# Layer norm by halves in a two-layer decoder trunk: squares about each half's own mean, and an earlier transpose

## The chip, the cores and the metric

The kernel runs on one core of a Trainium2 chip. The metric is the device time of one execution in microseconds (us). Before the change it is 533.94 us, the median of 3 runs (533.82 to 534.5).

## The reference

Two post-norm layers over 256 tokens of width 1024, in fp32. Layer 0 has a mixer with sparse attention, layer 1 one with stick-breaking attention; each layer ends in a hierarchical mixture of experts. Behind the mixer and behind the experts stands a layer norm, four in all:

```python
def layer_norm(x, g, b):
    xf = x.astype(jnp.float32)
    mu = jnp.mean(xf, axis=-1, keepdims=True)
    var = jnp.mean(jnp.square(xf - mu), axis=-1, keepdims=True)
    return ((xf - mu) * lax.rsqrt(var + LN_EPS) * g + b).astype(x.dtype)
...
    for layer in range(DEPTH):
        ...
        x = layer_norm(DEEPNORM_ALPHA * x + mix, ln_mix_g[layer], ln_mix_b[layer])
        ffn = hierarchical_moe(x, moe_w_grp[layer], moe_b_grp[layer], ...)
        x = layer_norm(DEEPNORM_ALPHA * x + ffn, ln_ffn_g[layer], ln_ffn_b[layer])
```

The experts of a token are chosen from logits of the normed `x` (a group of four, then two experts in it).

## The kernel before, in words

The 256 tokens are two tiles of 128, one token in each partition, with the 1024 features along the free axis. A tile's features are handled in two halves of 512, because the result of a product fills one bank of PSUM (`acc`, 128 x 512). TensorE (PE) makes all products and transposes; VectorE (DVE) and ScalarE (ACT) move and convert results; SyncE (SP) issues the transfers of weights.

A norm has two helpers. `ln_sum` (L340) adds the residual: one `scalar_tensor_tensor` (L344) for each half writes `r = ALPHA*r + acc` and, as a second small instruction, the half's sum to a column of the tile `st`; L346 makes the negative mean of both. `ln_rstd` (L349) lets ACT square each half about the common mean (L353, with the sum of the squares as a second small instruction), then come small DVE steps on one element of each partition: L354 and L355 make the variance, ACT takes Ln and Exp (L356, L357), and L358 to L360 are one Newton step for the inverse root. A norm is made at four places:

- **the route** (`ln_route`, L446, once in each layer's mixer). `proj` adds the last products of the output projection (`out_proj`, L396 to L398), first for tile 0, then for tile 1, half by half. Between them PE transposes the summed `x` of a tile (`mk_xT`, L420, by `transp4`, L309, four 128 x 128 transposes in one PSUM buffer, copied to `rT` by DVE, L314, or ACT, L316). `logits` (L459) multiplies `rT` with the router's weights (L464), copies the four partial results (`part`, L469) and sums them by a product with `sel` (L470). `finish` (L475) corrects the logits by mean and inverse root (L478, L479), `norm` (L481) scales `x` on ACT, and `router` (L945, first step L973) ranks the logits. The gather of tokens (L1231) waits for the ranks. The PSUM buffers of the transposes come from a pool of two.
- **the middle** (`ln_tile`, L363), behind the experts of layer 0, tile 0 and then tile 1. Between `ln_sum` and `ln_rstd` DVE makes `u` of 1024 elements (L372). For tile 0 PE runs 30 small keep-warm products (L370, L327). L381 makes the normed halves, `done` transposes each (L309) and ACT copies them to `xT` (L316). PE then multiplies `xT` with a block of layer 1's weights (`proj_whole`, L254) before it goes on to layer 1's other projections (L266 to L268).
- **the end** (`fin`, L1559), both tiles together, with `u` in L1569 and the result in L1574 and L1575.

Each engine works its instructions off in the order of its own list. The order within a list is set by a scheduler when the program is built. `tc.issue_after(i)` holds what is issued in it behind instruction `i` in that order; `last[...]` keeps such instructions.

A second copy of the program with dense experts follows behind a branch and is not executed here.

Of the kernel before, what the change touches and what calls it, by code (L numbers as in the profile page):

```python
# [9 lines left out]
F32 = mybir.dt.float32  # L10
# [4 lines left out]
OP = mybir.AluOpType  # L15
# [18 lines left out]
def trunk(ctx, tc, io):  # L34
# [301 lines left out]
    def after_ln():  # L336
        with tc.issue_after(last["A"]), tc.issue_after(last["V"]):
            yield

    def ln_sum(r, accs):  # L340

        st = sm.tile([128, 8], F32, name="lnst")
        for h in range(2):
            V.scalar_tensor_tensor(r[:, h * 512:h * 512 + 512], r[:, h * 512:h * 512 + 512], ALPHA, accs[h],  # L344
                                   op0=OP.mult, op1=OP.add, accum_out=st[:, h:h + 1])
        last["m"] = V.tensor_scalar(st[:, 2:3], st[:, 0:1], st[:, 1:2], -1.0 / D, op0=OP.add, op1=OP.mult).ins  # L346
        return st

    def ln_rstd(r, accs, st):  # L349

        nmu, ve, rs, nt = st[:, 2:3], st[:, 3:4], st[:, 4:5], st[:, 5:6]
        for h in range(2):
            last["S"] = A.activation(accs[h], r[:, h * 512:h * 512 + 512], AF.Square, bias=nmu, accum_out=st[:, 6 + h:7 + h]).ins  # L353
        V.tensor_scalar(nt, st[:, 6:7], 1.0 / D, EPS, op0=OP.mult, op1=OP.add)  # L354
        V.tensor_scalar(ve, st[:, 7:8], 1.0 / D, nt, op0=OP.mult, op1=OP.add)  # L355
        A.activation(rs, ve, AF.Ln)  # L356
        last["A"] = A.activation(rs, rs, AF.Exp, scale=-0.5).ins  # L357
        V.tensor_scalar(ve, ve, -0.5, None, op0=OP.mult)  # L358
        V.tensor_scalar(nt, ve, rs, rs, op0=OP.mult, op1=OP.mult)
        last["R"] = V.tensor_scalar(rs, nt, 1.5, rs, op0=OP.add, op1=OP.mult).ins  # L360
        return rs

    def ln_tile(t, r, accs, gb, u, done, warm=0):  # L363


        gt, bt = gb[:, 0], gb[:, 1]
        with tc.issue_after(last["V"] if t else last["lo"]):
            st = ln_sum(r, accs)
        if warm:
            keep_warm(warm, pmt)  # L370
        with (tc.issue_after(last["V"]) if t else nullcontext()):
            last["u"] = V.scalar_tensor_tensor(u, r, st[:, 2:3], gt, op0=OP.add, op1=OP.mult).ins  # L372
        with tc.issue_after(last["u"]):
            rs = ln_rstd(r, accs, st)
        if warm:
            p = pmt()
            for _ in range(2):
                PE.matmul(p[:, 0:256], identf, rs.to_broadcast([128, 256]), start=True, stop=True)
        for h in range(2):
            hs = slice(h * 512, h * 512 + 512)  # L380
            last["V"] = V.scalar_tensor_tensor(r[:, hs], u[:, hs], rs, bt[:, hs], op0=OP.mult, op1=OP.add).ins  # L381
            done(h)
# [37 lines left out]
    def mk_xT(x, xT, t, pool=None, dve=0):  # L420
        for g in range(2):
            mk_xT_half(x, xT, t, g, pool, g < dve)
# [23 lines left out]
    def ln_route(l, x, a, oT, wo, xo, rT, pool):  # L446
# [40 lines left out]
        sts[0] = ln_sum(x[:, 0], a[0])  # L487
        proj(1, (0,))
        mk_xT(x, rT, 0, pool, 1)
        proj(1, (1,))  # L490
        logits(0)
        rss[0] = ln_rstd(x[:, 0], a[0], sts[0])
        norm(0)
        sts[1] = ln_sum(x[:, 1], a[1])
        with tc.issue_after(last["m"]):
            mk_xT(x, rT, 1, pool, 2)
            last["E"] = last["C"]
        rss[1] = ln_rstd(x[:, 1], a[1], sts[1])
        logits(1)
        finish(0)  # L500
        finish(1)
# [1001 lines left out]
    def program(sparse):  # L1503
# [55 lines left out]
        def fin(t, a, gb, u):  # L1559
# [7 lines left out]
            for k in range(NT):  # L1567
                with tc.issue_after(last["m"]):
                    V.scalar_tensor_tensor(box1[k][1], x[:, k], sts[k][:, 2:3], gb[:, 0], op0=OP.add, op1=OP.mult)  # L1569
            rs = [ln_rstd(x[:, k], box1[k][0], sts[k]) for k in range(NT)]  # L1570
            for k in range(NT):
                for h in range(2):
                    hs = slice(h * 512, h * 512 + 512)
# [79 lines left out]
```

## Time and profile before

| | us |
|---|---|
| median of 3 runs | 533.94 |
| the profiled execution | 533.85 |
| its span, first to last instruction | 531.9 |
| PE busy | 501.4 (94%) |
| DVE busy | 289.5 (54%) |
| ACT busy | 220.8 (42%) |

The span is the profiled execution without what lies around the first and the last instruction, 1.95 us. The busy times overlap, since the engines work side by side; PE's matmuls are pipelined, so its 94% is no measure of how near it is to its peak. Times in rows are counted from the start of the span.

### The profile page before, as it was taken

The numbers are of one execution on the slowest core, as the hardware profiler recorded it, in microseconds if no ns is written. First come the engines' busy times: TensorE is split into PE (matmuls) and PEld (weight loads), VectorE is DVE, ScalarE is ACT, GpSimd is POOL, SyncE is SP. The second block draws the span as 40 slices with busy tenths as digits, with TensorE's granted clock in tenths as the row PEclk, the third lists the DMA queues.
The fourth block names the chain that finished last, engine by engine and source line by source line (L and its number), as shares of the span: only waits on it lengthen the run. The fifth ranks groups of instructions, "written<-read, shape, count | busy, mean of one in ns | idle before, by whom it ended". The sixth has DMA issues, their size and how long they took to land.

```text
span 531.9 us, 8516 instructions
## 1 busy us (share of the span) xinstructions
PE 501.4 (94%) x3201; PEld 316.4 (59%) x3201; DVE 289.5 (54%) x824; ACT 220.8 (42%) x433; POOL 7.6 (1%) x18
## 2 busy tenths in 40 slices
PE   8899989999999999999899999999999999999980
PEld 6687656676676354543354996898777454363320
DVE  5878796849669621221166555555648861141125
ACT  4545645547556121121144347556747321131022
POOL 1000000000020000000000000000002000000000
PEclk9999999999999999999999999999999999999995
DMA  8999500009938999999997980003976599999952
GB/s 243 381 429 429 217 0 1 1 0 393 412 152 322 415 363 335 421 422 422 432 430 307 370 341 1 0 1 147 427 297 238 224 394 342 402 423 419 427 217 84
DMA packets 25536, 150.02 MB, mean 282 GB/s; under 512 B 3472, under 2 KB 4112, under 8 KB 14992
## 3 DMA queue, kind: packets, MB, share of 16 engines
q1 hardware_dynamic: 25488, 149.41, 70.1%
q8 instruction: 27, 0.44, 0.3%
q14 instruction: 21, 0.17, 0.1%
HBM read 148.35 MB, written 1.05 MB: 281 GB/s over the span
## 4 chain that ended last, share of the span: by engine, by line
PE 82%; DVE 9%; ACT 4%; DMA 2%; issue 1%; SPq 0%; ACTq 0%; DVEq 0%
PE pmt L1264 16%; PE pmt L1296 9%; PE pmt L1231 4%; PE acc L1305 3%; PE acc L246 3%; PE acc L245 3%; PE acc L398 3%; PE acc L244 3%; PE acc L396 3%; PE acc L397 3%; PE acc L254 3%; DMA wb<-w 2%; PE acc L268 2%; PE acc L266 2%; PE acc L267 2%; PE z L880 2%
## 5 line engine op out<-in xcount | busy, mean ns | idle before, releaser
L1264 PE MATMUL pmt<-wgu,xg 128*64 128x512 f32 (+1 forms) x512 | 92.8, 595 | 0.0
L1264 PEld LDWEIGHTS pmt<-wgu,xg 128*64 128x64 f32 (+1 forms) x512 | 27.2, 123 | 52.9 <-issue 50.8
L190 ACT ACTIVATE wh<-wb 128x1024 fp32r<-128x1024 f32 (+2 forms) x44 | 41.1, 944 | 37.4 <-PE acc L267 19.7
L193 DVE TENSOR_TENSOR wl<-wb,wh 128x512 fp32r<-128x512 f32 (+1 forms) x72 | 45.1, 660 | 19.0 <-ACT wh L190 18.9
L1296 PE MATMUL pmt<-wd,hT 128*64 128x512 f32 (+1 forms) x256 | 53.9, 597 | 0.9 <-ACT hT L1280 0.9
L198 DVE TENSOR_TENSOR yl<-pmt,yh 128x512 fp32r<-128x512 f32 x20 | 13.8, 690 | 47.5 <-ACT yh L190 47.5
L246 PE MATMUL acc<-wl,xhl 128*128 128x512 f32 (+1 forms) x96 | 37.7, 395 | 1.5 <-DVE wl L193 1.5
L244 PE MATMUL acc<-wh,xhl 128*128 128x512 f32 (+1 forms) x96 | 37.3, 389 | 1.4 <-ACT wh L190 1.4
L245 PE MATMUL acc<-wh,xhl 128*128 128x512 f32 (+1 forms) x96 | 37.0, 386 | 0.0
L1272 DVE SCALAR_TENSOR_TENSOR hh<-pmt,cs,silu 128x256 f32<-128x256 f32 x12 | 5.8, 484 | 56.8 <-ACT silu L1270 56.8
L1270 ACT ACTIVATE silu<-pmt 128x256 f32<-128x256 f32 x12 | 4.6, 384 | 76.1 <-PE pmt L1264 76.1
L190 ACT ACTIVATE yh<-pmt 128x512 fp32r<-128x512 f32 x20 | 11.9, 597 | 55.9 <-PE pmt L1296 55.9
L1296 PEld LDWEIGHTS pmt<-wd,hT 128*64 128x64 f32 (+1 forms) x256 | 15.3, 123 | 27.0 <-issue 24.9
L1231 PEld LDWEIGHTS pmt<-Poh,xhl 128*128 128x128 f32 x192 | 24.4, 188 | 5.3 <-issue 3.2
L266 PE MATMUL acc<-xhl,wh 128*128 128x256 f32 x96 | 27.5, 287 | 0.0
L1231 PE MATMUL pmt<-Poh,xhl 128*128 128x256 f32 (+1 forms) x192 | 26.7, 292 | 0.3 <-DVE xg L1239 0.3
L268 PE MATMUL acc<-xhl,wl 128*128 128x256 f32 x96 | 26.9, 280 | 0.0
L267 PE MATMUL acc<-xhl,wh 128*128 128x256 f32 x96 | 26.8, 279 | 0.0
L398 PE MATMUL acc<-xol,oT 128*128 128x512 f32 x64 | 26.1, 412 | 0.0
L396 PE MATMUL acc<-xo,oT 128*128 128x512 f32 x64 | 25.9, 410 | 0.0
L397 PE MATMUL acc<-xo,oT 128*128 128x512 f32 x64 | 25.5, 401 | 0.0
L581 ACT ACTIVATE Pm<-pst,nm 128x128 f32<-128x128 f32 (+1 forms) x48 | 19.8, 419 | 10.7 <-DVE nm L579 9.5
(368 smaller groups left out, 984.0 us busy)
## 6 DMA issues: line engine op xcount, KB each, us to landing
wd<-wd SPq DMA_DIRECT2D x34, 1024.0 KB, 11.0
wgu<-wgu SPq DMA_DIRECT2D x64, 512.0 KB, 11.1
wgu<-wgu SPq DMA_DIRECT2D x14, 2048.0 KB, 12.1
wb<-w1s SPq DMA_DIRECT2D x6, 2048.0 KB, 19.1
wo<-wo SPq DMA_DIRECT2D x4, 2048.0 KB, 16.2
wgu<-wgu SPq DMA_DIRECT2D x8, 1024.0 KB, 7.2
wb<-w SPq DMA_DIRECT2D x3, 2048.0 KB, 22.0
wb<-w SPq DMA_DIRECT2D x2, 1024.0 KB, 8.9
```

Source lines behind the costliest of these rows:

```text
L190: A.activation(dst_h, src, AF.Copy)
L193: V.tensor_tensor(dst_l[:, i], src[:, i], dst_h[:, i].bitcast(F32), OP.subtract)
L244: PE.matmul(a[t][:, :n], xh[:, cc, ts], wh[:, c, :n], start=(cc == 0), stop=False)
L245: PE.matmul(a[t][:, :n], xl[:, cc, ts], wh[:, c, :n], start=False, stop=False)
L246: PE.matmul(a[t][:, :n], xh[:, cc, ts], wl[:, c, :n], start=False, stop=(cc == NCH - 1))
L266: PE.matmul(o, wh[:, c, fs], xh[:, cc], start=(cc == 0 and f % 2 == 0), stop=False, skip_group_check=True)
L396: PE.matmul(a[t][h], oc[:, 0, ts], wh[:, hs], start=first, stop=False)
L397: PE.matmul(a[t][h], oc[:, 1, ts], wh[:, hs], start=False, stop=False)
L398: PE.matmul(a[t][h], oc[:, 0, ts], wl[:, hs], start=False, stop=last)
L1231: PE.matmul(p[:, 0:w], src[:, t, c * 128:c * 128 + 128], P[:, t, u * 128:u * 128 + w], start=(t == 0 and src is xh), stop=(t == 1 and src ...
L1264: PE.matmul(pg[r, :], g[:, c, BASE[u] + r.start:BASE[u] + r.stop], ws[k, c], start=(c == 0), stop=(c == NCH - 1), tile_position=(0, r.start))
L1296: PE.matmul(y[r, :], hT[:, fc, r], wd[k][:, fc, h * 512:h * 512 + 512], start=(fc == 0), stop=(fc == 1), tile_position=(0, r.start))
```

## The change

`ln_half` takes the place of the two loops. It adds the residual of one half (L344 in the changed kernel too) and lets ACT square it at once (now L345) about that half's own mean: with scale -512 and the half's sum as bias, the square is 512 squared times the squared distance from the half's mean, and the factors 2^-18/D take that out again. `ln_mean` (L349) makes the common mean. `ln_rstd` joins the halves: L362 takes the difference of the sums, L363 squares it and adds EPS, and L364 and L365 add the two sums of squares. So four small steps stand where two stood, and the Squares no longer wait for the mean. This holds for all four norms.

In `ln_route` the first half of tile 1 (sum, Square and the four transposes with the copy to `rT`) is written between the two halves of the last products, and its second half behind `norm(0)`; mean and `ln_rstd` of tile 1 are held behind the copy of the second half's transposes.

```diff
+    def ln_half(r, accs, st, h):
+        rh = r[:, h * 512:h * 512 + 512]
+        last["h"] = V.scalar_tensor_tensor(rh, rh, ALPHA, accs[h], op0=OP.mult, op1=OP.add, accum_out=st[:, h:h + 1]).ins
+        last["S"] = A.activation(accs[h], rh, AF.Square, bias=st[:, h:h + 1], scale=-512.0, accum_out=st[:, 6 + h:7 + h]).ins
+
+    def ln_mean(st):
+        last["m"] = V.tensor_scalar(st[:, 2:3], st[:, 0:1], st[:, 1:2], -1.0 / D, op0=OP.add, op1=OP.mult).ins
+
     def ln_sum(r, accs):
         st = sm.tile([128, 8], F32, name="lnst")
         for h in range(2):
-            V.scalar_tensor_tensor(r[:, h * 512:h * 512 + 512], r[:, h * 512:h * 512 + 512], ALPHA, accs[h],
-                                   op0=OP.mult, op1=OP.add, accum_out=st[:, h:h + 1])
-        last["m"] = V.tensor_scalar(st[:, 2:3], st[:, 0:1], st[:, 1:2], -1.0 / D, op0=OP.add, op1=OP.mult).ins
+            ln_half(r, accs, st, h)
+        ln_mean(st)
         return st
 
-    def ln_rstd(r, accs, st):
-        nmu, ve, rs, nt = st[:, 2:3], st[:, 3:4], st[:, 4:5], st[:, 5:6]
-        for h in range(2):
-            last["S"] = A.activation(accs[h], r[:, h * 512:h * 512 + 512], AF.Square, bias=nmu, accum_out=st[:, 6 + h:7 + h]).ins
-        V.tensor_scalar(nt, st[:, 6:7], 1.0 / D, EPS, op0=OP.mult, op1=OP.add)
-        V.tensor_scalar(ve, st[:, 7:8], 1.0 / D, nt, op0=OP.mult, op1=OP.add)
+    def ln_rstd(st):
+        ve, rs, nt = st[:, 3:4], st[:, 4:5], st[:, 5:6]
+        V.tensor_scalar(nt, st[:, 0:1], st[:, 1:2], 1.0 / D, op0=OP.subtract, op1=OP.mult)
+        V.tensor_scalar(ve, nt, nt, EPS, op0=OP.mult, op1=OP.add)
+        V.tensor_scalar(nt, st[:, 6:7], 2.0 ** -18 / D, ve, op0=OP.mult, op1=OP.add)
+        V.tensor_scalar(ve, st[:, 7:8], 2.0 ** -18 / D, nt, op0=OP.mult, op1=OP.add)
         A.activation(rs, ve, AF.Ln)
...
         sts[0] = ln_sum(x[:, 0], a[0])
         proj(1, (0,))
         mk_xT(x, rT, 0, pool, 1)
+        sts[1] = sm.tile([128, 8], F32, name="lnst")
+        ln_half(x[:, 1], a[1], sts[1], 0)
+        mk_xT_half(x, rT, 1, 0, pool, True)
         proj(1, (1,))
         logits(0)
-        rss[0] = ln_rstd(x[:, 0], a[0], sts[0])
+        rss[0] = ln_rstd(sts[0])
         norm(0)
-        sts[1] = ln_sum(x[:, 1], a[1])
-        with tc.issue_after(last["m"]):
-            mk_xT(x, rT, 1, pool, 2)
+        ln_half(x[:, 1], a[1], sts[1], 1)
+        with tc.issue_after(last["h"]):
+            mk_xT_half(x, rT, 1, 1, pool, True)
             last["E"] = last["C"]
-        rss[1] = ln_rstd(x[:, 1], a[1], sts[1])
+        with tc.issue_after(last["C"]):
+            ln_mean(sts[1])
+            rss[1] = ln_rstd(sts[1])
         logits(1)
```

The calls in `ln_tile` and `fin` only lose the arguments `r` and `accs`. In the changed kernel L356 and L357 are L366 and L367, L358 to L360 are L368 to L370, L372 is L382, L378 is L388, L381 is L391, L396 to L398 are L406 to L408, L464 is L474, L469 and L470 are L479 and L480, L478 and L479 are L488 and L489, L973 is L988, L1569 is L1584; L309, L314, L316, L254 and L266 keep their numbers.

The order of the lists, at three places. First ACT in the middle norm. The numbers of `acc` and `lnst` tell the tiles apart: the lower is tile 0, the higher tile 1. Before:

```order
L353 ACTIVATE acc_1878,lnst_2757<-xn_127,lnst_2757 128x512
L353 ACTIVATE acc_1879,lnst_2757<-xn_127,lnst_2757 128x512
L356 ACTIVATE lnst_2757<-lnst_2757 128x1
L357 ACTIVATE lnst_2757<-lnst_2757 128x1
L316 ACTIVATE xT_2756<-pmt_2806 128x4x128
L316 ACTIVATE xT_2756<-pmt_2813 128x4x128
L353 ACTIVATE acc_1880,lnst_2828<-xn_127,lnst_2828 128x512
L353 ACTIVATE acc_1881,lnst_2828<-xn_127,lnst_2828 128x512
L356 ACTIVATE lnst_2828<-lnst_2828 128x1
```

And in the changed kernel:

```order
L345 ACTIVATE acc_1882,lnst_2761<-xn_127,lnst_2761 128x512
L345 ACTIVATE acc_1883,lnst_2761<-xn_127,lnst_2761 128x512
L366 ACTIVATE lnst_2761<-lnst_2761 128x1
L367 ACTIVATE lnst_2761<-lnst_2761 128x1
L345 ACTIVATE acc_1884,lnst_2834<-xn_127,lnst_2834 128x512
L345 ACTIVATE acc_1885,lnst_2834<-xn_127,lnst_2834 128x512
L316 ACTIVATE xT_2760<-pmt_2812 128x4x128
L316 ACTIVATE xT_2760<-pmt_2819 128x4x128
L366 ACTIVATE lnst_2834<-lnst_2834 128x1
```

The two Squares of tile 1 stood behind the two copies to `xT` and stand ahead of them now.

Second PE in the route of layer 0, behind the transposes of tile 0. `acc_1356` is the second half of tile 1, `xo` and `xol` are the split weights, `oT` the attention's output. Before:

```order
L309 MATMUL pmt_1664<-identf_79,xn_127 128x128 x4
L396 MATMUL acc_1356<-xo_1352,oT_1442 128x512
L397 MATMUL acc_1356<-xo_1352,oT_1442 128x512
L398 MATMUL acc_1356<-xol_1338,oT_1442 128x512
L396 MATMUL acc_1356<-xo_1352,oT_1503 128x512
```

And in the changed kernel:

```order
L309 MATMUL pmt_1666<-identf_79,xn_127 128x128 x4
L406 MATMUL acc_1356<-xo_1352,oT_1442 128x512
L407 MATMUL acc_1356<-xo_1352,oT_1442 128x512
L408 MATMUL acc_1356<-xol_1338,oT_1442 128x512
L309 MATMUL pmt_1675<-identf_79,xn_127 128x128 x4
L406 MATMUL acc_1356<-xo_1352,oT_1503 128x512
```

Four transposes of tile 1 stand among the twelve products of its second half.

Third DVE in the same route, from the sum of tile 1's second half on. `lnst_1642` and `lpart` with the lower number are tile 0. Before:

```order
L344 SCALAR_TENSOR_TENSOR xn_127,lnst_1705<-xn_127,acc_1356 128x512
L469 COPY lpart_1691<-acc_1682 128x128
L346 TENSOR_SCALAR lnst_1705<-lnst_1705 128x1
L314 COPY rT_1603<-pmt_1709 128x4x128
L314 COPY rT_1604<-pmt_1715 128x4x128
L354 TENSOR_SCALAR lnst_1705<-lnst_1705 128x1
L478 SCALAR_TENSOR_TENSOR lgq_1767<-bsw_126,lnst_1642,acc_1682 128x20
L355 TENSOR_SCALAR lnst_1705<-lnst_1705 128x1
L479 SCALAR_TENSOR_TENSOR lg_1617<-lgq_1767,lnst_1642,bsw_126 128x20
L469 COPY lpart_1746<-acc_1730 128x128
```

And in the changed kernel:

```order
L344 SCALAR_TENSOR_TENSOR xn_127,lnst_1672<-xn_127,acc_1356 128x512
L479 COPY lpart_1702<-acc_1693 128x128
L488 SCALAR_TENSOR_TENSOR lgq_1771<-bsw_126,lnst_1642,acc_1693 128x20
L314 COPY rT_1604<-pmt_1718 128x4x128
L349 TENSOR_SCALAR lnst_1672<-lnst_1672 128x1
L362 TENSOR_SCALAR lnst_1672<-lnst_1672 128x1
L489 SCALAR_TENSOR_TENSOR lg_1617<-lgq_1771,lnst_1642,bsw_126 128x20
L363 TENSOR_SCALAR lnst_1672<-lnst_1672 128x1
L479 COPY lpart_1750<-acc_1734 128x128
L364 TENSOR_SCALAR lnst_1672<-lnst_1672 128x1
L365 TENSOR_SCALAR lnst_1672<-lnst_1672 128x1
```

One copy to `rT` is gone from here, the first correction of the logits stands ahead of the other, and the mean and three small steps stand between it and the second `lpart`.

## Rows read from the trace of the kernel before

**Rows 1.** The page, its first part (busy time, share, instructions) and its fourth (shares of the chain that ended last):

```profile
PE 501.4 (94%) x3201; PEld 316.4 (59%) x3201; DVE 289.5 (54%) x824; ACT 220.8 (42%) x433; POOL 7.6 (1%) x18
...
PE 82%; DVE 9%; ACT 4%; DMA 2%; issue 1%; SPq 0%; ACTq 0%; DVEq 0%
```

**Rows 2.** The chain of waits in order of time, around the middle norm: start, length, engine, what.

```profile
272.07 1.53 ACT acc L353 x4
275.04 1.11 PE pmt L378 x4
...
277.28 7.13 PE acc L254 x16
...
285.53 7.13 PE acc L254 x16
```

**Rows 3.** The view of waits, PE alone, from 277 to 400 us: who waited for whom, us in total, times, the longest.

```profile
PE acc L254 <- ACT xT L316: 0.4, 2, 0.2
PE z L880 <- ACT sph L190: 0.3, 1, 0.3
```

**Rows 4.** The timeline of the middle norm, from the first sum of tile 0 to the second Square of tile 1: start, length, engine, line, operation, out<-in, count, and in brackets the idle time before it with its releaser.

```profile
270.91 0.09 DVE L344 DVE_READ_ACCUMULATOR xn<-xn,acc 128x1 f32 x1
...
271.71 0.08 DVE L344 DVE_READ_ACCUMULATOR xn<-xn,acc 128x1 f32 x1
...
272.07 0.69 ACT L353 ACTIVATE acc<-xn,lnst 128x512 f32<-128x512 f32 x1 [2.41 <-DVE lnst L346]
272.07 1.28 DVE L372 SCALAR_TENSOR_TENSOR lnu<-xn,lnst,lngb 128x1024 f32<-128x1024 f32 x1
...
273.28 0.15 DVE L354 TENSOR_SCALAR lnst<-lnst 128x1 f32<-128x1 f32 x1
...
273.63 0.22 DVE L355 TENSOR_SCALAR lnst<-lnst 128x1 f32<-128x1 f32 x1 [0.20 <-ACT acc L353]
273.88 0.20 ACT L356 ACTIVATE lnst<-lnst 128x1 f32<-128x1 f32 x1 [0.28 <-DVE lnst L355]
...
274.93 1.42 DVE L381 SCALAR_TENSOR_TENSOR xn<-lnu,lnst,lngb 128x512 f32<-128x512 f32 x2
...
275.99 1.13 PE L309 MATMUL pmt<-identf,xn 128*128 128x128 f32 x8
...
276.62 1.13 ACT L316 ACTIVATE xT<-pmt 128x512 f32<-128x512 f32 x2 [2.31 <-PE pmt L309]
276.87 0.08 DVE L344 DVE_READ_ACCUMULATOR xn<-xn,acc 128x1 f32 x1
...
277.28 7.13 PE L254 MATMUL acc<-wb,xT 128*128 128x512 f32 x16 [0.15 <-ACT xT L316]
...
277.85 0.69 ACT L353 ACTIVATE acc<-xn,lnst 128x512 f32<-128x512 f32 x1
...
278.57 0.67 ACT L353 ACTIVATE acc<-xn,lnst 128x512 f32<-128x512 f32 x1
```

**Rows 5.** The timeline of layer 0's route, from the transposes of tile 0 to the router's first step.

```profile
151.16 1.03 PE L309 MATMUL pmt<-identf,xn 128*128 128x128 f32 x8
...
151.97 0.69 DVE L314 COPY rT<-pmt 128x512 f32<-128x512 f32 x1
...
152.73 0.39 PE L396 MATMUL acc<-xo,oT 128*128 128x512 f32 x1
...
154.56 0.39 PE L398 MATMUL acc<-xol,oT 128*128 128x512 f32 x1
...
156.14 1.30 DVE L314 COPY rT<-pmt 128x512 f32<-128x512 f32 x2
...
157.50 0.42 PE L464 MATMUL acc<-rT,wr 128*32 128x128 f32 x8 [0.19 <-DVE lnst L354]
...
157.87 0.20 ACT L356 ACTIVATE lnst<-lnst 128x1 f32<-128x1 f32 x1 [0.31 <-DVE lnst L355]
...
159.28 0.24 DVE L479 SCALAR_TENSOR_TENSOR lg<-lgq,lnst,bsw 128x20 f32<-128x20 f32 x1
...
159.56 0.32 DVE L973 TENSOR_TENSOR rge<-lg 128x160 bf16<-128x160 f32 x1
```

**Rows 6.** The timeline of layer 1's route: the last product, and the router's first step.

```profile
402.46 0.39 PE L398 MATMUL acc<-xol,oT 128*128 128x512 f32 x1
...
407.67 0.32 DVE L973 TENSOR_TENSOR rge<-lg 128x160 bf16<-128x160 f32 x1
```

**Rows 7.** The timeline of the end: `u` of both tiles, the first small step of both tiles, and Ln of both.

```profile
519.53 2.47 DVE L1569 SCALAR_TENSOR_TENSOR lnu<-xn,lnst,lngb 128x1024 f32<-128x1024 f32 x2
...
521.91 0.21 DVE L354 TENSOR_SCALAR lnst<-lnst 128x1 f32<-128x1 f32 x2
...
522.35 0.34 ACT L356 ACTIVATE lnst<-lnst 128x1 f32<-128x1 f32 x2 [0.62 <-DVE lnst L355]
```

**Rows 8.** The table by stretches at the end: the stretch, its length, the busy time of each engine with its instructions, then the granted clock of PE as a share of full speed, the share of the DMA engines and GB/s.

```profile
520.00:520.25 0.25, 0.00 (x0) 0.00 (x0) 0.25 (x1) 0.25 (x3) 0.00 (x0) 0.50 0.00 0
```

**Rows 9.** The timeline of PE: the keep-warm products at the start of the program, those of the middle norm, and the last products of the program.

```profile
1.06 3.38 PE L327 MATMUL pmt<-oneb 128*128 128x256 bf16 x15 [1.06 <-DVE oneb L105]
...
271.13 3.45 PE L327 MATMUL pmt<-oneb 128*128 128x256 bf16 x30
...
515.31 2.22 PE L1311 MATMUL acc<-yb,ST 128*128 128x512 f32 x8
```

More of the change, by code (lines that the diff above doesn't have):

```diff
@@ L373, in ln_tile @@
         with tc.issue_after(last["u"]):
-            rs = ln_rstd(r, accs, st)
+            rs = ln_rstd(st)
         if warm:
@@ L1569, in fin @@
                     V.scalar_tensor_tensor(box1[k][1], x[:, k], sts[k][:, 2:3], gb[:, 0], op0=OP.add, op1=OP.mult)
-            rs = [ln_rstd(x[:, k], box1[k][0], sts[k]) for k in range(NT)]
+            rs = [ln_rstd(sts[k]) for k in range(NT)]
             for k in range(NT):
```

## The prediction, made before the changed kernel ran

> **What bounds the kernel now.** I read the page's shares and the chain of waits first, then the chain in order of time, then the timeline around each of the four places where a norm is made. The page shows TensorE (PE) busy for 94% of the span and 82% of the chain on it [rows 1]: what PE does elsewhere is untouched, so the change counts only where PE waits for a norm. There are four such places, two routes, the middle and the end. The chain shows the middle one plainly: it runs through the Squares of tile 0 and the small products that wait for the root (L378), and then stays on PE (L254) to the next stage [rows 2]. A delay ahead of L254 is a delay of the program if nothing later has time to spare; in the stage behind it PE waits for no transfer, its two groups of waits are 0.4 and 0.3 us [rows 3].
>
> The profiled execution took 533.85 us, the median is 533.94: my sum is made on the trace and shifted by 0.09.
>
> **The middle norm (`ln_tile`, tile 0).** Before, the first Square starts at 272.07, behind the mean. Each half's sum is there at 271.00 and 271.79 (start and length of the two accumulator reads), so the new Squares can start at 271.05 and 271.84 and are done at about 272.7 [rows 4]. That is worth nothing: VectorE (DVE) works on `u` (L372) from 272.07 to 273.35, and the steps of `ln_rstd` stand behind it. Before, two steps followed it: L354 at 273.28, then L355 at 273.63, which waited for the second Square, and Ln at 273.88. Now there are four (L362 to L365), each waiting for the one before. One such step costs 0.25 (L355 to Ln [rows 4]): 273.28 + 4 x 0.25 = 274.28, so **+0.40** for Ln and all behind it.
>
> The larger term is ScalarE's (ACT) queue. Both Squares of tile 1 now stand ahead of the two copies `xT` (L316) of tile 0, and they stood behind them. The first of them needs the first sum of tile 1, made at 276.95 [rows 4]; with the 0.40 that is 277.35, so it starts at 277.40. One Square holds ACT for 0.72 (277.85 to 278.57), so the second starts at 278.12 and the first copy at 278.84, where it started at 276.62. L254 follows its copy by 0.66 and starts at 279.50 instead of 277.28: **+2.22**, the 0.40 included. Bounds: 0.40 if the copies were not held at all, 2.94 if one more Square's 0.72 came on top. I take 2.22: which work stands first on ACT is fixed, and each duration is of the same instruction.
>
> **The route of layer 0 (`ln_route`).** The first half's transposes of tile 1 move from behind the last product into the middle of that tile's second half. On PE they cost what they cost behind it: eight took 1.03, so four 0.5 [rows 5]. They also need a `pmt` buffer, of which there are two, and the `rT` copy that frees one ends at 152.66; PE comes to them at 152.73, so that wait is about nothing. The last product, which ended at T = 154.95 (154.56 + 0.39), ends **0.5** later. Bounds: 0 (only moved) and 1.03.
>
> Behind it the tail gets one `rT` copy fewer, half of 1.30. Before, both copies were done at 157.44, T + 2.49, and Ln came at T + 2.92. Now the single copy stands behind `part`'s matmul of tile 0, the last transpose and L488, and ends at about T + 2.4, an estimate from the lengths above. Behind it stand L349, L362, L489, L363, the second `part` copy, which needs the logits' 0.42, then L364 and L365: 0.42 + 3 x 0.25 gives Ln at about T + 3.57. From Ln on, Exp, L369 and L370 need 1.05 (273.88 to 274.93 in the middle [rows 4]) and from L489 to the router's first step (before: L973) it is 0.28 more (159.28 to 159.56 [rows 5]), 1.33 in all, where 1.69 passed before. So the router starts at T + 4.9, and started at T + 4.61: **+0.3**, bounds -0.65 (a copy saved, nothing added) and +1.0 (four steps of 0.25, all open). Layer 0 in all: **+0.8**.
>
> **The route of layer 1.** The same move: 0.5 on PE. There T was 402.85 and the router started at T + 4.82 [rows 6], so the tail adds 0.1. **+0.6**. Same bounds. Both routes pass their delay on whole, since the gather waits for the router's ranks.
>
> **The end (`fin`).** The Squares end earlier, but L1569 holds DVE until 522.00 [rows 7]. From the first step behind it (521.91) Ln was 0.44 away, and now it comes after L363, L364 and L365 of tile 0 with two steps of tile 1 in the gaps. Two steps that do not need each other took 0.21 together [rows 7], so a step in a gap costs about 0.06: 3 x 0.25 in all, **+0.3**, bounds 0 and 0.8 (five steps of 0.25).
>
> The Trainium skill, "VectorE: DVE Perf Modes", section "The DRAIN you can't avoid", speaks against added steps more strongly: the next operation does not start until the pipe is empty, so one should keep their number low, whether or not they depend on each other. By that rule the end would cost 0.8 and the sum would be 0.5 higher; the pair in 0.21 in this trace is against it for steps that do not depend on each other.
>
> Nothing moves on the queues of SyncE and GpSimd. The two extra steps in the middle's tile 1 are hidden behind 7.13 us of L254.
>
> Sum: 2.22 + 0.8 + 0.6 + 0.3 = 3.9; 533.85 + 3.9 + 0.09 = **537.8 us**, 0.7% slower. A measurement tells about 0.2% (1.07 us) from no change.
>
> **Rivals.**
> - *The TensorE clock falls in the middle.* After its last matmul ends at 517.53 PE does nothing, and the granted clock is 0.50, the 1.2 GHz level, at 520.00 [rows 8, 9]. In the middle PE would stand still from 277.52 (transposes, 277.12 + 0.40) to 279.50, 1.98 us [rows 4], after a first stop of 0.86. That is less than the 2.47 within which it fell at the end, but near. If it falls, the program's start shows the price: 15 keep-warm matmuls took 3.38 us there, 30 of the same shape 3.45 at 271.13 [rows 9], so running in again costs 3.38 - 1.73 = 1.65: 537.8 + 1.65 = 539.5 us. The Trainium skill, "TensorE: Matmul & The Clock Gate", Part 4, says that transposes do not count as busy the way matmuls do. By that rule the stop would begin at the end of L378's matmuls, 276.55 with the delay, and last 2.95, and the clock would fall; the trace of before does not show whether it holds. Chance 0.33.
> - *The tail of the routes gains.* If the saved copy (0.65) is all that is felt there, each route gives +0.5 - 0.65 and the sum is 2.22 + 0.3 - 0.3 = 2.2: 536.1 us. Against it: Ln stands behind the added steps on the same queue. Chance 0.08.
> - *Not slower: layer 1's weights take the delay up.* Place: the projection of layer 1, from L266 on. If a block of `w1s` landed there over 3 us later than PE comes to it, the 2.2 and the 0.8 ahead of it would vanish in that wait, and 0.6 + 0.3 would be left: 534.8 us, no change that can be told. It decides from a wait of PE for DMA of 3 us in that stretch; the view of waits shows none [rows 3]. Chance 0.05.
> - *The change does nothing to the Squares.* Their bias is the half's own sum, so they can start early; and as shown that early start is covered by `u` in any case. This lies inside the forecast.
>
> **How the numbers follow.** Forecast 0.50, alone 536.8 to 538.9 (the bounds of the four terms, which will not all fall on one side). Clock 0.33, tail 0.08, taken up 0.05, and 0.04 for what I don't see. The range 536.0 to 540.6 takes in forecast and clock and most of the tail case, and leaves out the rest, about a tenth. Faster by over 0.2%: 0.03 (part of the last two). Within: 0.04. Slower: 0.93.
>
> **What would show it.** In the middle: the Squares of tile 0 start at 1.0 us before their old place relative to the sums, Ln 0.4 later, ACT idle before two L345 and only then L316, and L254 about 2.2 later relative to the first sum; clock 1.00 there, or 0.50 in the rival. In the routes: four L309 among the products, the last product 0.5 later, Ln over 3.5 us behind it. At the end Ln about 0.75 behind `u`. I am wrong if L254 starts within 1 us of its old distance from the sums, or if the router starts earlier behind the last product.

## The result, and the profile after

The changed kernel took 541.1 us, the median of 4 runs (539.39 to 543.11); the kernel before took 534.22 beside it. The ratio is 1.013, with a 95% interval of 1.0107 to 1.0153. So it is slower, as forecast, but by 6.9 us and not by 3.9, and 0.5 us above the upper end of the range. Two executions far from all others, 2747.53 us in the first experiment below and 986.12 of the kernel before, are in no ratio. The profiled execution took 540.73 (span 538.8, before 531.9). The page's shares hardly moved; they answer to [rows 1]:

```profile
PE 504.4 (94%) x3201; PEld 317.1 (59%) x3201; DVE 292.5 (54%) x840; ACT 220.3 (41%) x433; POOL 7.5 (1%) x18
...
PE 83%; DVE 9%; ACT 3%; DMA 3%; issue 1%; SPq 0%; DVEq 0%; ACTq 0%
```

Shares don't show where time went. A ledger by stages does: the same landmarks in both timelines, and the differences between them. It adds up to the spans.

| stage, by its first and last landmark | before | changed | difference | forecast |
|---|---|---|---|---|
| start to the first sum of layer 0's route | 147.96 | 146.61 | -1.35 | 0 |
| first sum to the end of the last product (T) | 6.99 | 7.70 | +0.71 | +0.5 |
| T to the router's first step | 4.61 | 5.26 | +0.65 | +0.3 |
| router to the first sum of the middle | 110.75 | 112.05 | +1.30 | 0 |
| first sum to L254 | 6.97 | 9.26 | +2.29 | +2.22 |
| L254 to the first sum of layer 1's route | 119.84 | 121.57 | +1.73 | 0 |
| first sum to the router of layer 1 | 10.55 | 11.28 | +0.73 | +0.6 |
| router to the first sum of the end | 108.98 | 109.12 | +0.14 | 0 |
| first sum of the end to the last instruction | 15.25 | 15.95 | +0.70 | +0.3 |

The first stage is not the change's: over all 17 profiles taken it lies between 146.6 and 148.95, whatever the kernel. The two stages with +1.30 and +1.73 were forecast at nothing, and both hold a stretch in which the clock was low. The table by stretches has the granted clock in the column behind the engines:

```profile
247.75:251.00 3.25, 3.25 (x13) 0.74 (x13) 0.00 (x0) 0.00 (x0) 0.00 (x0) 0.50 1.02 420
...
278.00:281.75 3.75, 1.83 (x10) 1.10 (x9) 3.46 (x10) 2.48 (x6) 0.00 (x0) 1.00 0.99 422
281.75:285.25 3.50, 3.50 (x5) 1.35 (x4) 3.03 (x8) 2.39 (x5) 0.00 (x0) 0.51 0.99 426
285.25:290.00 4.75, 4.75 (x16) 2.30 (x15) 0.70 (x2) 0.00 (x0) 0.00 (x0) 1.00 0.82 352
```

Half clock, the 1.2 GHz level, twice while PE has work: behind 247.7 in the first mixture of experts (MoE), and behind 281.8. Both lower a run's mean clock, which is the granted clock averaged over its span as a share of the 2.4 GHz level. From 278.00 to 281.75 PE was busy for 1.83 of 3.75 us, and the clock fell behind that. The timeline of the middle norm, which answers to [rows 4]:

```profile
272.23 0.08 DVE L344 DVE_READ_ACCUMULATOR xn<-xn,acc 128x1 f32 x1
...
274.59 0.21 DVE L362 TENSOR_SCALAR lnst<-lnst 128x1 f32<-128x1 f32 x1
274.83 0.21 DVE L363 TENSOR_SCALAR lnst<-lnst 128x1 f32<-128x1 f32 x1
275.15 0.21 DVE L364 TENSOR_SCALAR lnst<-lnst 128x1 f32<-128x1 f32 x1
275.47 0.21 DVE L365 TENSOR_SCALAR lnst<-lnst 128x1 f32<-128x1 f32 x1
275.72 0.20 ACT L366 ACTIVATE lnst<-lnst 128x1 f32<-128x1 f32 x1 [1.77 <-DVE lnst L365]
...
278.83 0.69 ACT L345 ACTIVATE acc<-xn,lnst 128x512 f32<-128x512 f32 x1 [2.67 <-DVE xn L344]
...
279.55 0.67 ACT L345 ACTIVATE acc<-xn,lnst 128x512 f32<-128x512 f32 x1
...
280.25 1.06 ACT L316 ACTIVATE xT<-pmt 128x512 f32<-128x512 f32 x2
...
280.88 8.83 PE L254 MATMUL acc<-wb,xT 128*128 128x512 f32 x16 [1.92 <-ACT xT L316]
```

This is the forecast picture: four steps behind `u`, both Squares of tile 1 ahead of the copies, PE waiting 1.92 us for the copy. What is new stands in the last row: the sixteen products took 8.83 and not 7.13 [rows 4], since the clock fell 0.9 us after they began. Layer 0's route (answers to [rows 5]) and the last product and router of layer 1 ([rows 6]):

```profile
151.56 0.66 PE L309 MATMUL pmt<-identf,xn 128*128 128x128 f32 x4
...
153.91 0.40 PE L408 MATMUL acc<-xol,oT 128*128 128x512 f32 x1
...
155.96 0.69 DVE L314 COPY rT<-pmt 128x512 f32<-128x512 f32 x1
156.57 0.20 DVE L349 TENSOR_SCALAR lnst<-lnst 128x1 f32<-128x1 f32 x1
...
156.81 0.62 DVE L489 SCALAR_TENSOR_TENSOR lg<-lgq,lnst,bsw 128x20 f32<-128x20 f32 x1
157.36 0.20 DVE L363 TENSOR_SCALAR lnst<-lnst 128x1 f32<-128x1 f32 x1
...
157.99 0.21 DVE L365 TENSOR_SCALAR lnst<-lnst 128x1 f32<-128x1 f32 x1
...
158.24 0.20 ACT L366 ACTIVATE lnst<-lnst 128x1 f32<-128x1 f32 x1 [2.31 <-DVE lnst L365]
...
159.57 0.32 DVE L988 TENSOR_TENSOR rge<-lg 128x160 bf16<-128x160 f32 x1
...
408.32 0.40 PE L408 MATMUL acc<-xol,oT 128*128 128x512 f32 x1
...
413.73 0.32 DVE L988 TENSOR_TENSOR rge<-lg 128x160 bf16<-128x160 f32 x1
```

T is 154.31. The one copy left ends at T + 2.34, Ln starts at T + 3.93, where I had T + 2.4 and T + 3.57. And the end ([rows 7]):

```profile
528.12 0.21 DVE L363 TENSOR_SCALAR lnst<-lnst 128x1 f32<-128x1 f32 x1
528.24 0.20 DVE L362 TENSOR_SCALAR lnst<-lnst 128x1 f32<-128x1 f32 x1
528.43 0.21 DVE L364 TENSOR_SCALAR lnst<-lnst 128x1 f32<-128x1 f32 x1
...
528.75 0.21 DVE L365 TENSOR_SCALAR lnst<-lnst 128x1 f32<-128x1 f32 x1
...
529.00 0.20 ACT L366 ACTIVATE lnst<-lnst 128x1 f32<-128x1 f32 x1 [2.50 <-DVE lnst L365]
...
530.21 0.74 DVE L1589 SCALAR_TENSOR_TENSOR xn<-lnu,lnst,lngb 128x512 f32<-128x512 f32 x1
530.87 0.20 DVE L370 TENSOR_SCALAR lnst<-lnst 128x1 f32<-128x1 f32 x1
```

Ln is 0.88 behind the first step, before 0.44 [rows 7]; a step of tile 1 (L370) stands between two halves of the result (L1589, before L1574), where before nothing did:

```profile
523.46 2.73 DVE L1574 SCALAR_TENSOR_TENSOR xn<-lnu,lnst,lngb 128x512 f32<-128x512 f32 x4
```

### The profile page after: what moved, and what is told of

Its sections match the earlier page's. It is cut to its first block, busy times and chain, and to the rows that moved or that the text cites. A ratio compares the mean times of both kernels' runs of the same rounds, so it can differ in the third digit from the quotient of the medians.

```text
span 538.8 us, 8538 instructions
## 1 busy us (share of the span) xinstructions
PE 504.4 (94%) x3201; PEld 317.1 (59%) x3201; DVE 292.5 (54%) x840; ACT 220.3 (41%) x433; POOL 7.5 (1%) x18
## 4 chain that ended last, share of the span: by engine, by line
PE 83%; DVE 9%; ACT 3%; DMA 3%; issue 1%; SPq 0%; DVEq 0%; ACTq 0%
PE pmt L1279 15%; PE pmt L1311 9%; PE pmt L1246 5%; PE acc L246 3%; PE acc L1320 3%; PE acc L245 3%; PE acc L408 3%; PE acc L254 3%; PE acc L244 3%; PE acc L406 3%; PE acc L407 3%; DMA wgu<-wgu 2%; PE acc L268 2%; PE acc L266 2%; PE acc L267 2%; PE acc L229 2%
## 5 line engine op out<-in xcount | busy, mean ns | idle before, releaser
L1279 PE MATMUL pmt<-wgu,xg 128*64 128x512 f32 (+1 forms) x512 | 94.2, 601 | 0.0
L1311 PE MATMUL pmt<-wd,hT 128*64 128x512 f32 (+1 forms) x256 | 55.5, 605 | 0.9 <-ACT hT L1295 0.9
L266 PE MATMUL acc<-xhl,wh 128*128 128x256 f32 x96 | 27.5, 287 | 0.0
L406 PE MATMUL acc<-xo,oT 128*128 128x512 f32 x64 | 26.1, 413 | 0.0
L408 PE MATMUL acc<-xol,oT 128*128 128x512 f32 x64 | 26.0, 412 | 0.0
```

The costliest lines, as they stand in the source:

```text
L266: PE.matmul(o, wh[:, c, fs], xh[:, cc], start=(cc == 0 and f % 2 == 0), stop=False, skip_group_check=True)
L406: PE.matmul(a[t][h], oc[:, 0, ts], wh[:, hs], start=first, stop=False)
L408: PE.matmul(a[t][h], oc[:, 0, ts], wl[:, hs], start=False, stop=last)
L1279: PE.matmul(pg[r, :], g[:, c, BASE[u] + r.start:BASE[u] + r.stop], ws[k, c], start=(c == 0), stop=(c == NCH - 1), tile_position=(0, r.start))
L1311: PE.matmul(y[r, :], hT[:, fc, r], wd[k][:, fc, h * 512:h * 512 + 512], start=(fc == 0), stop=(fc == 1), tile_position=(0, r.start))
```

## The experiments

My theory: each term is where its stage shows it, and the rest is the clock, which falls because PE stops ahead of L254. The rivals: the falls have nothing to do with that stop, or something else of the change brings them.

**The copies first.** The changed kernel, tile 1's Squares behind tile 0's copies in the middle (`X` is the last copy to `xT`):

```
+        with (tc.issue_after(last["X"]) if hold else nullcontext()):
+            last["S"] = A.activation(accs[h], rh, AF.Square, ...).ins
```

> The changed kernel, with one thing put back: in the middle norm the two Squares of tile 1 are held behind the two xT copies of tile 0 on ScalarE. Theory A (ScalarE's order holds L254): L254 starts 0.5 us later than before relative to the first sum of tile 0 (the four small steps alone), not 2.3; TensorE's stop ahead of it falls from 1.9 to about 0.15 us; the granted clock stays at 1.00 from the middle on; time 537.6 to 538.4 us, 2.7 to 3.5 below the changed kernel's 541.1. Rival B (the clock falls wherever it likes, the middle's order has nothing to do with it): L254 moves the same, but runs still show mean clocks of 0.972 to 0.986 and the time is about 539.3. Rival C (L254 is held by something else, the small steps or the late sum of tile 1): no gain, 541.

538.11 us (537.97 without the far execution), ratio 1.0059 (1.0035 to 1.0083) against 1.013, so 3 to 4 us of the loss gone. One of its timeline's rows:

```profile
281.44 7.13 PE L254 MATMUL acc<-wb,xT 128*128 128x512 f32 x16 [0.16 <-ACT xT L316]
```

L254 is 7.51 behind the first sum, the stop is 0.16, the products take 7.13 again. So of the 2.29 the four steps cost 0.54 and the place of the two Squares on ACT 1.75. Theory A holds for the middle. But its profile has half clock in three other places (64.8, 249.1, 498.3), so B has a part: there are falls that the middle does not make.

**PE filled, and filled with transposes.** The changed kernel, ten more instructions on PE ahead of the second four transposes:

```
+        for _ in range(fill):
+            PE.matmul(p[:, 0:256], oneb, oneb.unsqueeze(1).to_broadcast([128, 2, 128]), ...)
         for i, s_ in enumerate(srcs):
             last["T"] = PE.transpose(...)
```

`fill` is 10 there and 0 elsewhere. In the second version the added line is

```
+            PE.transpose(p[:, 0:128], srcs[0], identf)
```

> The changed kernel, with ten keep-warm products (128x256, bf16) ahead of the second four transposes of tile 0 in the middle norm, so that TensorE works in most of its 1.9 us stop ahead of L254; all orders on ScalarE and VectorE stay. Theory A (a stop of TensorE makes the clock fall, and the delay of L254 is ScalarE's): L254 starts at the same 9.2 to 9.3 us behind the first sum, no half-clock stretch behind the middle, L254's first eight take 3.6 us and not 5.4; 0.9 to 1.7 us less than the changed kernel, 539.4 to 540.2. Rival B (the fall has nothing to do with the stop): mean clock and time as in the changed kernel, 541. Rival C (the fill itself delays the transposes): L254 later by up to 1.1 us, 541 to 542.

> The changed kernel, with ten extra transposes (128x128) ahead of the second four of tile 0 in the middle norm, in place of the ten keep-warm products of the run with filled TensorE. All five profiles of kernels with the stop of about 2 us ahead of L254 have a half-clock stretch behind it, the filled one has none. Theory A (any work of TensorE holds the clock): clock 1.00 through the middle, L254 9.2 to 9.3 us behind the first sum and its sixteen products 7.1 us. Rival B (transposes do not hold it): a half-clock stretch begins between 0.5 us ahead of L254 and 1.5 us behind its start, as without a fill, and the mixer behind it is 1.7 us longer.

539.81 us, ratio 1.01 (1.0075 to 1.0125), and 538.81, 1.0089 (1.0062 to 1.0116). A row of the timeline and one of the table by stretches, first of the fill with products:

```profile
281.31 7.13 PE L254 MATMUL acc<-wb,xT 128*128 128x512 f32 x16 [0.93 <-ACT xT L318]
```

```profile
281.75:290.00 8.25, 8.00 (x25) 3.90 (x24) 5.23 (x13) 3.47 (x8) 0.00 (x0) 1.00 0.97 417
```

then of the fill with transposes:

```profile
281.29 7.13 PE L254 MATMUL acc<-wb,xT 128*128 128x512 f32 x16 [0.83 <-ACT xT L318]
```

```profile
282.00:290.00 8.00, 7.75 (x24) 3.71 (x24) 5.08 (x12) 3.50 (x8) 0.00 (x0) 1.00 0.94 401
```

In both L254 is still 9.26 or 9.27 behind the first sum, but the clock is 1.00 and the stage behind it takes 119.86 and 119.88, as before the change. So the delay of L254 and the clock are two prices, 2.29 and 1.73, and only the second goes when PE is kept at work. Transposes kept the clock as well as products, in the one profile with them.

**The routes alone.** The changed kernel with the old mean, Squares and two steps in the middle and at the end:

```
-            st = ln_sum(r, accs)
+            st = ln_sum0(r, accs)
...
-            rs = ln_rstd(st)
+            rs = ln_rstd0(r, accs, st)
```

`ln_sum0` and `ln_rstd0` are the functions of the kernel before; `fin` has the same edit.

> The changed kernel's two routes, with the middle norm and the end as they were before (Squares about the common mean, two small steps). Theory A (the terms add up): the routes cost what the trace of the changed kernel shows, 0.71 + 0.65 in layer 0 and 0.73 in layer 1, so 534.2 + 2.1 = 536.3 us; the granted clock is 1.00 up to the end, mean 0.989. Rival B (the clock's other falls, such as that in the first MoE at 247.7, come with the routes' order): mean clocks of 0.980 to 0.986 and 537.2 to 539. Rival C (the routes' delay is taken up by a wait behind them): 534.2 to 535.

537.0 us, ratio 1.0046 (1.0024 to 1.0067), 2.5 us, where A had 2.1; mean clocks from 0.979 to 0.991, so A's steady clock did not come. The stages of the routes are those of the changed kernel (12.96 and 11.28), the middle and the end those of before (6.96 and 15.16). The stage behind the first route takes 110.39 and not 110.75: the first MoE gives 0.36 of the delay back, here and (0.29 to 0.37) in every profile with the new route order whose clock stays up there. Why, I don't know.

**The routes' old order.** The changed kernel, no early transposes, both `rT` copies of tile 1 behind its mean:

```
-        ln_half(x[:, 1], a[1], sts[1], 0)
-        mk_xT_half(x, rT, 1, 0, pool, True)
...
+        sts[1] = ln_sum(x[:, 1], a[1])
+        with tc.issue_after(last["m"]):
+            mk_xT(x, rT, 1, pool, 2)
```

> The changed kernel's norms everywhere (each half's squares about its own mean, four small steps), with the routes' work in the order of before: no early transposes of tile 1, both rT copies behind its mean. Theory A: the middle costs 2.3 + a clock fall of 0.9 to 1.7, the end 0.6, a route between -0.3 (one Square less ahead of Ln) and +0.4 (two more steps), so 534.2 + 2.3 + 1.3 + 0.6 +- 0.6 = 537.8 to 539.0 us, and the last product of a route ends where it did before (7.0 us behind the first sum). Rival B (the early transposes are free, the delay of the routes is that of the four steps): 540 to 541.

538.41 us, ratio 1.0067 (1.0044 to 1.009). Last product and router of layer 0:

```profile
154.39 0.39 PE L408 MATMUL acc<-xol,oT 128*128 128x512 f32 x1
...
159.43 0.32 DVE L983 TENSOR_TENSOR rge<-lg 128x160 bf16<-128x160 f32 x1
```

T is 6.98 behind the first sum and the router at T + 4.65: the new norm alone costs layer 0's route 0.03 (layer 1's 0.25), the new order the other 1.33. The clock fell in the middle here too.

**The mean not held.** The changed kernel, without the hold of mean and steps behind the `rT` copy:

```
-        with tc.issue_after(last["C"]):
-            ln_mean(sts[1])
-            rss[1] = ln_rstd(sts[1])
+        ln_mean(sts[1])
+        rss[1] = ln_rstd(sts[1])
```

> The changed kernel, with the mean and the four steps of tile 1 in the routes no longer held behind the rT copy of its second half. Theory A (half of the routes' cost is the last product that comes 0.7 later, the other half the steps that stand behind the copy): the steps start in VectorE's idle time ahead of the copy, Ln of tile 1 comes 0.6 to 1.0 us earlier behind the last product, the router 0.3 to 0.6 earlier in each route, and the time is 0.6 to 1.2 below the changed kernel at equal clock; the last product stays 0.7 late. Rival B (the router waits for the logits of the second half, not for Ln): Ln is earlier and the router is not, no gain.

Last product and router of layer 0:

```profile
154.22 0.40 PE L408 MATMUL acc<-xol,oT 128*128 128x512 f32 x1
...
159.38 0.32 DVE L987 TENSOR_TENSOR rge<-lg 128x160 bf16<-128x160 f32 x1
```

Layer 0's route is 0.51 shorter (router at T + 4.76), layer 1's only 0.10, where A had 0.3 to 0.6 in each. So most of the tail in layer 0 was the hold. The time doesn't show it: 541.41 us, ratio 1.0119 (1.0082 to 1.0157). Part of that can be seen in its timeline:

```profile
272.25 1.28 DVE L382 SCALAR_TENSOR_TENSOR lnu<-xn,lnst,lngb 128x1024 f32<-128x1024 f32 x1 [0.68 <-DMA lngb<-lng]
```

`u` of the middle waited 0.68 for its row of gains. Two of the later profiles of the changed kernel or its versions have that wait too (0.69 and 0.32), the five profiles with the middle norm of before have it in none; what makes the transfer late is open.

**Only a stop, in the kernel before.** Five Squares that nobody uses ahead of the copies:

```
+                if t == 0 and h == 0:
+                    for _ in range(5):
+                        last["D"] = A.activation(u[:, 0:512], x[:, 0, 0:512], AF.Square).ins
```

> The kernel before, with five extra Squares of 128x512 on ScalarE ahead of the two xT copies of tile 0 in the middle norm (their result is not used): nothing of the change, only a stop of TensorE of about 2 us ahead of L254. Theory A: L254 starts 1.9 us later, the clock falls behind the stop in this profile and costs up to 1.7 us: 534.5 + 1.9 + 0.9 to 1.7 = 537.3 to 538.1. Rival B (a stop of that length by itself doesn't move the clock, something else of the change does): 536.4, mean clock as in the kernel before. Rival C (the delay is taken up behind the middle): 534.5.

539.02 us, ratio 1.0083 (1.006 to 1.0107). A row of its timeline and one of its table by stretches:

```profile
281.31 8.68 PE L254 MATMUL acc<-wb,xT 128*128 128x512 f32 x16 [2.97 <-ACT xT L317]
```

```profile
281.25:284.25 3.00, 2.94 (x4) 1.40 (x5) 1.33 (x5) 2.69 (x9) 0.00 (x0) 0.50 1.01 431
```

The stop became 2.97, not 2, since a Square of tile 1 got in between: L254 2.80 late. The clock fell and the stage behind took 1.58 more; 2.80 + 1.58 = 4.4, and the median is 4.3 above that of before. Nothing of the change is needed for it.

**A route meant to beat before.** Half means in the routes alone, old order, the second copy on ACT (`mk_xT(x, rT, 1, pool, 1)`), middle and end as before.

> A version meant to beat both: the kernel before, with each half's squares about its own mean in the two routes alone, no early transposes of tile 1, and the rT copy of its second half on ScalarE, which has one Square less to do there. Middle and end as before. Theory A (a route's end is set by VectorE, which holds two copies and the steps): the router starts 0.4 to 0.7 us earlier behind the last product than before (T + 4.61), 0.8 to 1.4 us less in all, 533.1 to 533.7. Rival B (the logits' path sets it: copy, products, part, products): the router at T + 4.5 to 4.7, 534.5 as before. Rival C (the extra steps cost more than the copy saves): up to 535.3.

534.61 us, ratio 1.0 (0.9981 to 1.0018): no gain. Layer 0's router came at T + 4.39 (0.22 earlier), layer 1's at T + 5.12 (0.30 later). Neither theory's numbers fit both. The root was done by then; a row of layer 1 shows what was waited for, the products of the logits, as in rival B. There the second copy stood behind a Square on ACT and started at T + 2.60, in layer 0 at T + 1.81:

```profile
405.80 0.57 ACT L316 ACTIVATE rT<-z 128x512 f32<-128x512 f32 x1
...
407.78 0.23 DVE L511 SCALAR_TENSOR_TENSOR lgq<-bsw,lnst,acc 128x20 f32<-128x20 f32 x1 [0.18 <-PE acc L503]
```

**The difference first.** As the copies first, with L362 and L363 ahead of `u`:

```
+            ln_diff(st)
+            with tc.issue_after(last["d"]):
                 last["u"] = V.scalar_tensor_tensor(u, r, ...)
```

> The changed kernel with tile 1's Squares behind the xT copies in the middle, and in the middle norm also the two steps on the means' difference (L362, L363) ahead of u on VectorE, where they need nothing but the two sums. Theory A (VectorE is one queue that is full there, so a step costs wherever it stands, and what is saved is the wait between dependent ones): u 0.4 to 0.6 later, Ln 0.1 to 0.3 earlier than in that run (4.1 behind the first sum), L254 7.2 to 7.4 behind the first sum against 7.5, and 6.97 in the kernel before. Rival B (the steps were dear because they stood behind u): Ln and L254 0.5 earlier, at 7.0. Rival C (they cost more ahead of u): L254 at 7.5 or later.

One execution, 538.57 us. The last step ahead of `u`, and `u` (L391 here):

```profile
274.32 0.21 DVE L364 TENSOR_SCALAR lnst<-lnst 128x1 f32<-128x1 f32 x1
274.45 1.28 DVE L391 SCALAR_TENSOR_TENSOR lnu<-xn,lnst,lngb 128x1024 f32<-128x1024 f32 x1
```

L254 is 7.17 behind the first sum, against 7.51 and 6.97, between what A and B said. The two steps put `u` 0.24 later, 2.01 behind the first sum and not 1.77, and took 0.57 from what follows it: ahead of `u`, which starts 0.13 behind the last of them, they cost less, but they are not free.

**The changed kernel again.** No edit; then two more profiles.

> The changed kernel itself, once more. The runs so far, fitted with one slope for the time at half clock, put it 4.5 +- 0.5 us over the kernel before at equal clock, and its first four runs had 8 us more of half clock than the runs of before. Theory A (only the stop in the middle adds half clock, the rest of those 8 us was chance): mean clocks of 0.980 to 0.989, median 539.6 to 540.4, a half-clock stretch behind the middle in the profile. Rival B (the change brings falls in other places too): mean clock again 0.972 to 0.986 and median 541.

> The changed kernel, one more profile. Theory A: half-clock stretches only behind the stop of the middle, behind the stops of the two MoEs, and in layer 0's attention. Rival B: one or more in another place, which would be the change's own.

542.79 us, ratio 1.0155 (1.0126 to 1.0184), so B and not A by time and clock, with runs from 539.55 (mean clock 0.986) to 543.92 (0.972). The first further profile is of an execution of 542.68 us:

```profile
248.00:251.00 3.00, 3.00 (x11) 0.68 (x11) 0.00 (x0) 0.00 (x0) 0.00 (x0) 0.50 1.02 418
...
282.25:285.25 3.00, 3.00 (x5) 1.15 (x4) 2.34 (x8) 2.28 (x5) 0.00 (x0) 0.50 1.02 437
...
500.75:503.75 3.00, 3.00 (x12) 0.73 (x12) 0.00 (x0) 0.00 (x0) 0.00 (x0) 0.50 1.02 419
```

Half clock in the middle and in both MoEs. The second, with the same expectation, took 540.48, with half clock in layer 0's attention and in the middle. So the places are those of A; the stops in the MoEs are in the kernel before too.

**The MoEs filled.** Eight keep-warm products in each MoE ahead of the products that wait for `yo`, a result of the experts, first in the kernel before, then in the changed one, then there with the middle's fill as well:

```
         def over_scatter(yo, ts=range(NT)):
+            keep_warm(8, pmt)
```

> A version meant to beat both: the kernel before, with eight keep-warm products (128x256, bf16) in each MoE ahead of L1354, where TensorE stands still for 1.07 us until yo is there. Four of the ten profiles so far have a half-clock stretch just behind that stop in the first MoE, four in the second, and the stage is 1.6 us longer where it has one. Theory A (a stop of TensorE brings these falls as it does in the middle, only not each time): no half-clock stretch between 240 and 255 nor between 490 and 502 any more, mean clock 0.987 to 0.991, median 0.8 to 1.4 us under the kernel before, 533.2 to 533.8. Rival B (the falls come from elsewhere): clocks and median as before, 534.6. Rival C (the fill delays the products behind it): 535.

> The changed kernel with eight keep-warm products ahead of L1369 in each MoE, as in the version that beat the kernel before. Three of the ten runs of the changed kernel had a mean clock of 0.972, which none of 49 of the kernel before had; no profile shows where. Theory A (those runs fall in the middle and in both MoEs): no run under 0.980 any more, the fall behind the middle stays, median 540 to 540.6, 0.8 to 1.5 us under the changed kernel. Rival B (the further falls are elsewhere, in layer 0 or around the middle): runs of 0.972 to 0.979 are still there, 541 to 542.5.

> The changed kernel with both fills, ten keep-warm products in the middle's stop and eight ahead of L1369 in each MoE. What is left over the kernel before with the same MoE fill (533.6) is what the change costs without the clock. Theory A (the stages add up: routes 1.36 + 0.73, less 0.36 that the first MoE gives back, middle 2.29, end 0.70): 533.6 + 4.7 = 538.3 us, between 537.8 and 538.8, mean clock 0.987 to 0.991. Rival B (half clock is still met elsewhere): under 0.985 and 539.5 or more.

| kernel | us | ratio, interval | lowest mean clock of its runs |
|---|---|---|---|
| before, MoEs filled | 533.62 | 0.9982 (0.9966 to 0.9998) | 0.984 |
| changed, MoEs filled | 540.31 | 1.0094 (1.0065 to 1.0123) | 0.983 |
| changed, MoEs and middle filled | 539.04 | 1.0084 (1.0056 to 1.0112) | 0.982 |

The first takes 0.8 us less than the kernel before, only just clear of noise (the interval ends at 0.9998). With the MoEs filled the changed kernel does what A said. With the middle filled too it came out between A (538.3) and B (539.5 or more): 5.4 above before with its MoEs filled, where the stages sum to 4.7. The stop of 1.07 us in the first MoE, in the kernel before and then in its filled version:

```profile
245.99 1.47 PE L1354 MATMUL acc<-yo,ST 64*128 64x512 f32 x4 [1.07 <-DVE yo L1347]
```

```profile
245.85 1.46 PE L1355 MATMUL acc<-yo,ST 64*128 64x512 f32 x4 [0.19 <-DVE yo L1347]
```

Over all 17 profiles: behind the stop of the middle the clock fell in 8 of the 8 that had it (1.92 us or more), and in none of the other 9. Behind the stop of 1.07 in the MoEs, which both kernels have, it fell in 7 of 14 in layer 0 and 6 of 14 in layer 1, and in none of the 3 with the fill. Nothing shows that the change makes these more frequent: it fell behind 6 of 14 such stops in the profiles with the stop of the middle, and behind 7 of 14 in those without.

## Why the prediction was wrong

**The sign and the mechanism of the stages were right.** ACT's order and the four steps hold L254 (2.29 against 2.22), the early Squares are worth nothing behind `u`, PE's last products are late by the transposes, the tails gain nothing. The rival that layer 1's weights take the delay up is out: with the clock at 1.00 the stage behind L254 takes 119.86, as before.

**The step that failed is the chance of the clock.** The prediction had the rival, its place, and its price (1.65; the stage was 1.73 longer), and gave it 0.33 because 1.98 us "is less than the 2.47 within which it fell at the end". That row says that a stop of that length was enough; it says nothing of shorter ones. Measured, it fell 8 times in 8. With it the sum was 539.5, inside the range; with the 1.1 of the terms below it is 540.6, the range's upper end, which left no room for both. The one execution in which I read the kernel before had no fall before its end, so it could not show that stops of 1.07 already bring one about every second time.

By the Trainium skill, "TensorE: Matmul & The Clock Gate", Part 4, transposes do not count as busy in the same way as matmuls, which would have moved the chance the right way. The fill with transposes speaks against that reason here, in its one profile: without it as work the stop would have lasted 2.9 us, and the clock stayed at 1.00. Without the stop of 1.92 (the copies first) or with work in it the clock did not fall there, and with a stop made in the kernel before it did.

**Four terms were too small, by 1.1 together.**
- *The last product of layer 0:* 0.71, not 0.5. I took half of the row with eight transposes in 1.03 [rows 5]; four by themselves took 0.66.
- *Layer 0's tail:* 0.65, not 0.3. The copy ended where I said, but L489 of tile 0, which I had counted as nothing, took 0.62 among the steps, and L364 and L365 each stand 0.31 or 0.32 behind the step before. Without the hold 0.51 goes.
- *The route of layer 1:* 0.73, not 0.6: 0.54 and 0.19, where I had 0.5 and 0.1.
- *The end:* 0.70, not 0.3. I took 0.25 for a step that waits for one, from L355 to Ln, which is DVE to ACT. From DVE to DVE it is 0.32 in most places (274.83, 275.15, 275.47); in the middle, too, Ln came 0.52 later and not 0.40. And the steps of tile 1 went in between, each for 0.12 (528.12, 528.24) where I had 0.06, one of them (L370) ahead of a half of the result.

The rule of the Trainium skill, "VectorE: DVE Perf Modes", section "The DRAIN you can't avoid", gave the end 0.8, nearer than mine. As a rule for every pair of steps it is not what the rows show: steps of two tiles stand 0.12 apart, steps that need each other 0.31 or 0.32. The section itself says that a next operation that is not held starts earlier.

**What is left.** The first MoE gives 0.36 back, the clock fell in it in this execution (stage 112.05; 110.38 in a profile without the fall), and the start was 1.35 shorter. Without the start, and without that fall, the stages sum to 6.6; the median lost 6.9, and 8.1 in the second measurement, so 0.3 to 1.5 is not accounted for. Three of 12 runs had a mean clock of 0.972 (of 62 of the kernel before none is under 0.979). The middle's fall on top of those in the MoEs, the three stretches in one profile, gives only 0.979; by the two means, 0.972 is an estimated 7 us more at half clock. The stretch from 64.8 to 71.7 in the profile of the copies first would be enough, but no profile shows a run of 0.972. With the MoEs filled no run is under 0.982, but only 6 of these had the stop of the middle, too few to be sure. Why a MoE's stop brings a fall in one execution and not in the next stays open, as does the length of the second MoE, which without a fall was 108.3 to 110.6 over the profiles, with no order by kernel that I can see.

## What to carry to other kernels

Before moving work ahead of a copy, ask who waits for the copy: two Squares of 0.7 us that nobody needed yet cost 1.75, and the stop they made on TensorE cost 1.7 more. Price a stop of TensorE twice, as the wait and as the clock behind it, and where the trace shows a fall after a longer stop only, take the shorter one as unknown, not as safe. Read more than one profile before calling a clock steady: a few keep-warm products in a stop that every execution has were worth 0.8 us (by the interval 0.1 to 1.8), while the change cost 7.

## What the runs showed that I had not expected

- The granted clock of the same program differs from one execution to the next: mean 0.979 to 0.991 over 62 runs of the kernel before (532.1 to 537.1 us). In four profiles of the changed kernel the stretches at half clock in both MoEs and in layer 0's attention are there in one and missing in the next; only that of the middle is in all four.
- Ten transposes of 128x128 (1.28 us) in the stop of the middle held the clock as ten products of 128x256 did (1.25 us), the transposes in one profile, the products in two.
- A transfer that is hidden in one execution can be waited for in the next: `lng`, 0.3 to 0.7 us in three of 17 profiles.
